# Sums for the conditioning vector: one run of four matmuls each, and units moved between stages of a four-layer trunk

## The chip, the cores and the metric

The kernel runs on one core of one Trainium2 chip. The metric is the device time of one execution in microseconds (us), the median of several runs. A core has five engines that run side by side and meet through semaphores: TensorE (PE in the profile, with its weight loads as PEld), VectorE (DVE), ScalarE (ACT), GpSimd (POOL) and SyncE (SP). SP here does nothing but issue transfers from memory, strictly in the order of the program: a transfer that must wait for a free buffer holds up all those behind it.

## The reference, cut to what matters

Four layers over 256 tokens of width 1024. Each layer has a token mixer (latent attention, causal convolution, pooling, latent attention) and a squared-ReLU MLP of width 4096. The part that the change touches is the modulation of each sub-layer by a conditioning vector `c`, called adaLN:

```
c_act = jax.nn.silu(c)
for i in range(DEPTH):
    mod = c_act @ ada_w[i] + ada_b[i]
    sh_m, sc_m, gt_m, sh_f, sc_f, gt_f = jnp.split(mod, 6, axis=-1)
    h = _rmsnorm(x, norm_g[i, 0]) * (1.0 + sc_m[:, None]) + sh_m[:, None]
    y = mixer(h)
    x = x + gt_m[:, None] * _rmsnorm(y, norm_g[i, 1])
    h = _rmsnorm(x, norm_g[i, 2]) * (1.0 + sc_f[:, None]) + sh_f[:, None]
    y = _sq_relu_mlp(h, ffn_w1[i], ffn_w2[i])
    x = x + gt_f[:, None] * _rmsnorm(y, norm_g[i, 3])
```

`ada_w` is 4 x 1024 x 6144 in float32, about 100 MB: a vector times a large matrix, once per layer, needed only when its sub-layer comes.

## The kernel before, in words

**The large products.** Weights arrive as 128 x 1024 float32 tiles (`raw`), are split into a high part (`hi`, ScalarE, L173) and a low part (`lo`, VectorE, L174), and TensorE multiplies high by high, high by low and low by high. An MLP goes through 16 chunks (`ffn`, L667): two halves of the hidden block (`h`, L652 and L655), its activation on ScalarE and VectorE (L704 to L710, which end in `gh` and `gl`), then one chunk later 24 matmuls into the output (`y`, L583, L586, L587). The last two chunks' `y` come at the end together, token tile by token tile.

**The conditioning vector.** Its weights are cut into units of 128 x 2048 (`araw`, 1 MB), eight units (k = 0 to 7) to a group, three groups to a layer; the first group is done at the start, 88 units are left. They run ahead of their use, wherever a table puts them: `MIX` and `FF` give for each sub-layer how many units go at each step or chunk, how many at the boundary ahead of it, and how many transfers are started ahead at its end. A unit is done in one of two ways (`ada`, L205):

- by TensorE (`ada_mm`, L260): four matmuls of 512 columns with 32 rows of output each, into the four quarters of one accumulator bank. All units at boundaries go this way.
- by VectorE: two multiply-adds of 128 x 1024 (L221 for the first of a group, then L223) into a pair of tiles, `acc`. All units in MLP chunks and most in the convolution go this way. The 128 partitions still have to be added up; that is one more `ada_mm`, with ones as the stationary side (`ada_flush`, L256), when the group is complete or the stage ends. I call this a sum.

When a group is complete its row is finished on VectorE (L240 to L244).

**What sets the order.** A scheduler orders the instructions of each compute engine by its own cost estimates and by the dependences. Before the change nothing ties the four matmuls of a unit or sum to each other: matmuls 0 and 1 read the first half of `acc`, 2 and 3 the second. SP's order is that of the program. There are 5 buffers for `raw`, 4 for `araw`; an `araw` buffer is free when the unit in it is summed.

**Boundaries** (L522). Between two sub-layers there is a chain: squares of `y`, a root on POOL, the residual, squares again, a root, a diagonal matrix, transposes, for token tile 0 and then tile 1. The units of the boundary are issued just after the last `y`. The wait for the second tile's `xa` (L406, L412) stands in the same chain.

**The end of an MLP.** At chunk 14 (`CF`) `ada_fetch(ahead)` starts several unit transfers in a row. After them SP issues the two tiles of `w2` for chunk 13, then those for chunks 14 and 15.

Of the kernel before, what the change touches and what calls it, by code (L numbers as in the profile page):

```python
# [51 lines left out]
def tile_trunk(ctx: ExitStack, tc: tile.TileContext, x, cT, pos, invf, ada_w, ada_bg,  # L52
# [20 lines left out]
    def bank(tag, name):  # L73
        return ps.tile([P, 512], F32, tag=tag, name=name, bufs={"y": 4, "h": 3, "ada": 1}[tag])
# [66 lines left out]
    def nosync(ins, behind):  # L141
        tc.add_manual_dep(ins.ins, behind.ins.name,
                          mybir.DependencyInfo(mybir.DependencyClass.NoSync,
                                               mybir.DependencyReason.DATA),
                          reason="after the chain")
# [58 lines left out]
    def ada(n, vec=()):  # L204
        for _ in range(n):  # L205
            if not units:
                ada_fetch(1)
            if not units:
                return
            i, g, k, raw = units.pop(0)  # L210
            if k == 0:
                grp.clear()
            if k in vec:
                ck = c_act[:, k, 0:1]
                first = "acc" not in grp
                if first:
                    grp["acc"] = sum_tiles()
                for h, acc in enumerate(grp["acc"]):
                    sl = slice(D * h, D * h + D)
                    if first:  # L220
                        V.tensor_scalar(acc, raw[:, sl], ck, None, ALU.mult)  # L221
                    else:
                        V.scalar_tensor_tensor(acc, raw[:, sl], ck, acc,  # L223
                                               op0=ALU.mult, op1=ALU.add)
            else:
                ada_mm(c_act[:, k, :], [raw[:, D * h:D * h + D] for h in range(2)],
                       k == KT - 1 and "acc" not in grp)
            if k == KT - 1:
                ada_flush(True)
                if defer[0] is None:  # L230
                    ada_row(i, g, grp["pt"])
                else:
                    defer[0].append((i, g, grp["pt"]))
# [22 lines left out]
    def ada_flush(stop=False):  # L256
        if "acc" in grp:
            ada_mm(ones_c, grp.pop("acc"), stop)

    def ada_mm(lhsT, raw, stop):  # L260
        first = "pt" not in grp
        if first:
            grp["pt"] = bank("ada", "adap")
        for j in range(4):
            mm = T.matmul(grp["pt"][32 * j:32 * j + 32, :], lhsT, raw[j // 2][:, HALF[j % 2]],
                          start=first, stop=stop)
            if gate["pe"] is not None:
                nosync(mm, gate["pe"])
        gate["ada"] = mm
# [907 lines left out]
    def pool(i, head, consts, units, ahead):  # L1177
# [87 lines left out]

    MIX = {
        0: ([2, 4, 2, 3, 3, 2], 0, 1),
        1: ([0, 0, 2, 0, 1, 2, 1, 0, 1], 2, 3),
        2: (2, 4, 3),
        3: ([0, 0, 0, 0, 0, 0], 0, 0),  # L1270
    }
    FF = {
# [3 lines left out]
        3: ([0] * NFC, 0, 0),  # L1276
    }
    qgs = cp.tile([P, q_g.shape[0], 3], F32, name="qgs")
# [139 lines left out]
```

## Time and profile before

| | us |
|---|---|
| runs shown | 1173.12, 1184.35, 1180.72 (median 1180.72) |
| the profiled execution | 1184.47 |
| its span, first to last instruction | 1182.6 |
| PE busy in the span | 1138.4 |
| DVE, ACT busy | 850.6, 645.3 |

The stages of the profiled execution: start and first attention to 150 us, MLP 0 to 342, convolution to 468, MLP 1 to 662, pooling to 690, MLP 2 to 882, second attention to 993, MLP 3 to the end. In the rows below, times are counted from the first instruction. A row of the timeline has its start, its length, engine, line, operation, output<-inputs, shape and count; what stands in brackets is the time that the engine stood idle just before, and what ended it. A float32 matmul shows as two instructions, so a sum or a unit on TensorE is "x8", half of one "x4". The end of a matmul is modelled; lengths on TensorE are therefore taken from start to start.

### The profile page before, as it was taken

How to read it: one execution, taken by the hardware profiler on the slowest of the kernel's cores; microseconds unless marked ns; L12 is line 12 of the kernel's file. 1: busy time of each engine (PE TensorE's matmuls, PEld its weight loads, DVE VectorE, ACT ScalarE, POOL GpSimd, SP SyncE). 2: the span in 40 equal slices, each digit the busy share in tenths (PEclk: the TensorE clock that was granted, in tenths of full speed). 3: DMA queues.
4: the chain of work that ended last, by engine and by line, in shares of the span. 5: the costliest groups of instructions: out<-in, count | busy, mean ns of one | idle time of the engine just before them, and what ended most of it. 6: DMA issues, size and time to landing. Idle time of an engine off the chain costs nothing. (4 is left out here: it accounts for less than half of the span.)

```text
span 1182.6 us, 17593 instructions
## 1 busy us (share of the span) xinstructions
PE 1138.4 (96%) x6706; PEld 923.5 (78%) x6706; DVE 850.6 (72%) x1197; ACT 645.3 (55%) x1145; POOL 54.1 (5%) x127
## 2 busy tenths in 40 slices
PE   7899999999999999999999999999997999999997
PEld 4667778788778867888887677878877878888886
DVE  3689787877766665787876778787876995755554
ACT  3355576556553244755564366555545675756553
POOL 1000010000010010000000110000011001000000
PEclk9999999999999988999999899999998999999999
DMA  9878759787617785778896479888644522766550
GB/s 332 304 290 311 298 208 347 270 329 290 245 53 236 256 322 213 272 272 351 315 343 256 187 278 364 311 311 323 246 134 157 170 81 80 250 199 191 183 193 35
DMA packets 73383, 290.00 MB, mean 245 GB/s; under 512 B 9986, under 2 KB 15234, under 8 KB 61012
## 3 DMA queue, kind: packets, MB, share of 16 engines
q1 hardware_dynamic: 70484, 280.44, 65.1%
q0 software_dynamic: 2816, 8.46, 2.0%
q8 instruction: 52, 0.85, 0.3%
q14 instruction: 31, 0.25, 0.1%
HBM read 286.57 MB, written 2.29 MB: 244 GB/s over the span
## 5 line engine op out<-in xcount | busy, mean ns | idle before, releaser
L174 DVE TENSOR_TENSOR lo<-raw,hi 128x1024 fp32r<-128x1024 f32 (+2 forms) x335 | 392.0, 1192 | 98.4 <-ACT hi L173 69.0
L173 ACT CAST hi<-raw 128x1024 fp32r<-128x1024 f32 (+2 forms) x335 | 335.1, 1028 | 78.6 <-PE y L587 39.4
L652 PE MATMUL h<-hT,hi 128*128 128x512 f32 x960 | 240.4, 392 | 0.0
L652 PEld LDWEIGHTS h<-hT,hi 128*128 128x128 f32 x960 | 175.8, 188 | 37.7 <-issue 3.4
L583 PE MATMUL y<-hi,gh 128*128 128x512 f32 x512 | 200.3, 393 | 1.5 <-ACT hi L173 1.5
L586 PE MATMUL y<-lo,gh 128*128 128x512 f32 x512 | 200.1, 391 | 0.2
L587 PE MATMUL y<-hi,gl 128*128 128x512 f32 x512 | 199.0, 390 | 0.0
L655 PEld LDWEIGHTS h<-hT,lo 128*128 128x128 f32 x960 | 131.0, 190 | 14.9 <-issue 5.9
L704 ACT COPY r<-h 128x256 f32<-128x256 f32 x120 | 44.5, 371 | 175.8 <-PE h L655 175.7
L655 PE MATMUL h<-hT,lo 128*128 128x256 f32 x960 | 136.0, 283 | 0.0
L223 DVE SCALAR_TENSOR_TENSOR acc<-araw,c_act,acc 128x1024 f32<-128x1024 f32 x106 | 130.7, 1279 | 0.4 <-DMA araw<-in_ada_w_dram 0.4
L583 PEld LDWEIGHTS y<-hi,gh 128*128 128x128 f32 x512 | 96.3, 188 | 22.8 <-ACT hi L173 2.4
L587 PEld LDWEIGHTS y<-hi,gl 128*128 128x128 f32 x512 | 96.1, 188 | 21.8 <-issue 0.8
L586 PEld LDWEIGHTS y<-lo,gh 128*128 128x128 f32 x512 | 96.4, 188 | 18.5 <-DVE lo L174 1.0
L705 DVE TENSOR_TENSOR r<-h,r 128x256 f32<-128x256 f32 x120 | 50.5, 421 | 39.8 <-ACT r L704 39.2
L710 DVE TENSOR_TENSOR gl<-r,gh 128x512 fp32r<-128x512 f32 x60 | 41.4, 690 | 50.2 <-ACT gh L709 50.2
L706 ACT ACTIVATE r<-r 128x512 f32<-128x512 f32 x60 | 37.9, 632 | 35.2 <-DVE r L705 35.2
L583 PE MATMUL y<-hi,hT 128*128 128x512 f32 x96 | 39.4, 412 | 0.0
L707 ACT ACTIVATE r<-r 128x512 f32<-128x512 f32 x60 | 37.9, 632 | 1.7
L586 PE MATMUL y<-lo,hT 128*128 128x512 f32 x96 | 38.8, 405 | 0.0
L587 PE MATMUL y<-hi,hT 128*128 128x512 f32 x96 | 38.6, 404 | 0.0
L709 ACT CAST gh<-r 128x512 fp32r<-128x512 f32 x60 | 37.2, 620 | 1.4
(257 smaller groups left out, 1486.8 us busy)
## 6 DMA issues: line engine op xcount, KB each, us to landing
raw<-in_w_dram SPq DMA_DIRECT2D x256, 512.0 KB, 5.8
araw<-in_ada_w_dram SPq DMA_DIRECT2D x96, 1024.0 KB, 6.4
raw<-in_w_pw_dram SPq DMA_DIRECT2D x24, 512.0 KB, 5.7
raw<-in_w_o_dram SPq DMA_DIRECT2D x16, 512.0 KB, 3.2
u<-ud SPq DMA_DIRECT2D x32, 132.0 KB, 2.8
raw<-in_w_ukv_dram SPq DMA_DIRECT2D x8, 512.0 KB
bc_g<-rowd POOLq DMA_DIRECT2D x8, 512.0 KB, 4.0
bc_a<-rowd POOLq DMA_DIRECT2D x7, 512.0 KB, 6.7
```

The source lines that it names most:

```text
L173: put(A.copy(h, raw), "act")
L174: put(V.tensor_tensor(l, raw, h.bitcast(F32), op=ALU.subtract), "dve")
L223: V.scalar_tensor_tensor(acc, raw[:, sl], ck, acc, op0=ALU.mult, op1=ALU.add)
L583: mm = T.matmul(o, ah, bh, start=start, stop=False, skip_group_check=True)
L586: T.matmul(o, ah, bl, start=False, stop=False, skip_group_check=True)
L587: return T.matmul(o, al, bh, start=False, stop=stop, skip_group_check=True)
L652: T.matmul(b, w(0, kk), pair[:, :, kk], start=(kk == 0), stop=False, skip_group_check=True)
L655: T.matmul(b[:, 0:S], w(1, kk), pair[:, 0, kk], start=False, stop=(kk == KT - 1), skip_group_check=True)
L704: A.copy(rf, hb[:, S:])
L705: V.tensor_tensor(rf, hb[:, 0:S], rf, op=ALU.add)
L706: A.activation(r, r, AF.Relu)
L710: gli = V.tensor_tensor(gl, g2, gh.bitcast(F32), op=ALU.subtract)
```

## The change

Two things. In `ada_mm` the four matmuls go in the order 2, 3, 0, 1, and each is tied behind the one before it, so that the scheduler keeps that order. And the table gives other numbers of units:

| | before | after |
|---|---|---|
| MLP 0, chunks (VectorE) | 15 | 17 |
| boundary into the convolution (TensorE) | 2 | 1 |
| convolution, its steps (VectorE) | 6 | 7 |
| convolution, after its taps (TensorE) | 1 | 0 |
| boundary into MLP 1 (TensorE) | 2 | 1 |
| MLP 1, chunks (VectorE) | 17 | 21 |
| boundary into the pooling, pooling (TensorE) | 4, 2 | 4, 2 |
| boundary into MLP 2 (TensorE) | 2 | 1 |
| MLP 2, chunks (VectorE) | 20 | 17 |

So 4 of the 88 units go from TensorE to VectorE. Since the groups now end elsewhere, the number of sums goes from 11 to 13: a new one at the end of MLP 0 and one at the end of the convolution. The numbers of transfers started ahead are as before.

```
         first = "pt" not in grp
         if first:
             grp["pt"] = bank("ada", "adap")
-        for j in range(4):
+        mm = None
+        for j in (2, 3, 0, 1):
+            prev = mm
             mm = T.matmul(grp["pt"][32 * j:32 * j + 32, :], lhsT, raw[j // 2][:, HALF[j % 2]],
                           start=first, stop=stop)
+            if prev is not None:
+                nosync(mm, prev)
             if gate["pe"] is not None:
                 nosync(mm, gate["pe"])
         gate["ada"] = mm
...
     FF = {
...
-        1: ([1, 1, 1, 2, 1, 1, 2, 1, 1, 2, 1, 1, 1, 1, 0, 0], 2, 4),
+        1: ([2, 1, 1, 2, 1, 2, 1, 2, 1, 2, 1, 2, 1, 2, 0, 0], 1, 4),
```

The lines of the new file from L272 on are four higher (L652 becomes L656), and L265 becomes L267.

TensorE, MLP 2, the last sum of the kernel (`adap<-acc`), ahead of the hidden block of chunk 15; before:

```order
L652 MATMUL h_8215<-hT,hi 128x512 x8
L655 MATMUL h_8215<-hT,lo 128x256 x6
L265 MATMUL adap<-acc,ones_c 32x512 x2
L655 MATMUL h_8215<-hT,lo 128x256 x2
L265 MATMUL adap<-acc,ones_c 32x512 x2
L652 MATMUL h_8234<-hT,hi 128x512 x8
```

and now:

```order
L656 MATMUL h_8217<-hT,hi 128x512 x6
L267 MATMUL adap<-acc,ones_c 32x512 x4
L656 MATMUL h_8217<-hT,hi 128x512 x2
L659 MATMUL h_8217<-hT,lo 128x256 x8
L656 MATMUL h_8236<-hT,hi 128x512 x8
```

The two pairs have become one run of four, which stands 8 matmuls earlier in the hidden block. All 13 sums now stand in runs of four; before, 9 of 11 were split.

ScalarE, the same place, from the activation of chunk 13 (`gh`) to that of chunk 14 (`hi` are weight tiles); before:

```order
L709 CAST gh<-r 128x512
L173 CAST hi<-raw 128x1024 x4
L704 COPY r<-h_8110 128x256
L173 CAST hi<-raw 128x1024
L704 COPY r<-h_8129 128x256
L706 ACTIVATE r<-r 128x512
L173 CAST hi<-raw 128x1024
L707 ACTIVATE r<-r 128x512
L173 CAST hi<-raw 128x1024
L709 CAST gh<-r 128x512
```

and now:

```order
L713 CAST gh<-r 128x512
L173 CAST hi<-raw 128x1024
L708 COPY r<-h_8112 128x256
L173 CAST hi<-raw 128x1024 x2
L708 COPY r<-h_8131 128x256
L710 ACTIVATE r<-r 128x512
L711 ACTIVATE r<-r 128x512
L713 CAST gh<-r 128x512
```

Seven weight casts stood between the two activations, three stand there now; none is left between the last `r` and `gh`.

SP, MLP 1, from the units of chunk 13 on (`araw` are units, `raw` MLP weights; `DVE_49` is a wait for VectorE); before:

```order
L197 DMA araw<-in_ada_w_dram 128x2048 x2
L200 DMA bg<-in_ada_bg_dram 4x1024 [waits DMAHW7_49]
L197 DMA araw<-in_ada_w_dram 128x2048 [waits DMAHW0_49,DVE_49]
L197 DMA araw<-in_ada_w_dram 128x2048 [waits DMAHW1_49,DVE_49]
L155 DMA raw<-in_w_dram 128x1024 [waits DMAHW2_49,Activation_49]
L155 DMA raw<-in_w_dram 128x1024 [waits DMAHW3_49,Activation_49]
```

and now:

```order
L197 DMA araw<-in_ada_w_dram 128x2048
L197 DMA araw<-in_ada_w_dram 128x2048 [waits DMAHW3_49,DVE_49]
L197 DMA araw<-in_ada_w_dram 128x2048 [waits DMAHW4_49,DVE_49]
L197 DMA araw<-in_ada_w_dram 128x2048 [waits DMAHW5_49,DVE_49]
L155 DMA raw<-in_w_dram 128x1024 [waits DMAHW6_49,Activation_49]
L155 DMA raw<-in_w_dram 128x1024 [waits DMAHW7_49,Activation_49]
```

Four transfers ahead as before. The last waits for the last unit of chunk 13 to be summed; that chunk had one unit and now has two.

## Rows read from the trace of the kernel before

**Rows 1.** The page, part 1: busy time of each engine.

```profile
PE 1138.4 (96%) x6706; PEld 923.5 (78%) x6706; DVE 850.6 (72%) x1197; ACT 645.3 (55%) x1145; POOL 54.1 (5%) x127
```

**Rows 2.** Groups by line, TensorE, units and sums: busy, mean ns, idle before.

```profile
L265 PE MATMUL adap<-araw,c_act 128*32 128x512 f32 x192 | 29.1, 607 | 0.0
L265 PE MATMUL adap<-acc,ones_c 128*32 128x512 f32 x88 | 21.9, 603 | 1.7 <-DVE acc L223 1.7
```

**Rows 3.** Timeline of TensorE, MLP 0, a sum in two pairs.

```profile
220.45 0.63 PE L652 MATMUL h<-hT,hi 128*128 128x512 f32 x2
221.02 1.05 PE L265 MATMUL adap<-acc,ones_c 128*32 128x512 f32 x4
...
222.67 1.05 PE L265 MATMUL adap<-acc,ones_c 128*32 128x512 f32 x4
223.65 0.73 PE L652 MATMUL h<-hT,hi 128*128 128x512 f32 x2
```

**Rows 4.** Timeline, the same place: VectorE's last units, TensorE's hidden block ahead.

```profile
217.30 4.87 DVE L223 SCALAR_TENSOR_TENSOR acc<-araw,c_act,acc 128x1024 f32<-128x1024 f32 x4
...
217.69 1.98 PE L652 MATMUL h<-hT,hi 128*128 128x512 f32 x8
219.50 0.76 PE L655 MATMUL h<-hT,lo 128*128 128x256 f32 x5
```

**Rows 5.** Timeline of TensorE, two sums that waited (MLP 0, MLP 2).

```profile
310.40 1.05 PE L265 MATMUL adap<-acc,ones_c 128*32 128x512 f32 x4 [0.69 <-DVE acc L223]
...
867.04 1.05 PE L265 MATMUL adap<-acc,ones_c 128*32 128x512 f32 x4 [0.98 <-DVE acc L223]
```

**Rows 6.** Timeline of TensorE, boundaries into MLP 0, convolution and MLP 2.

```profile
150.00 1.07 PE L265 MATMUL adap<-araw,c_act 128*32 128x512 f32 x8
150.99 0.48 PE L381 MATMUL hT_ps<-pick,shT 40*128 40x512 f32 x1
...
340.43 1.92 PE L265 MATMUL adap<-araw,c_act 128*32 128x512 f32 x16
342.29 0.48 PE L381 MATMUL hT_ps<-pick,shT 40*128 40x512 f32 x1
...
691.88 1.16 PE L395 MATMUL hT_ps<-dg,xa 128*128 128x128 f32 x8 [1.20 <-ACT dg L389]
```

**Rows 7.** Timeline of TensorE, the unit after the convolution's taps.

```profile
436.16 1.44 PE L265 MATMUL adap<-araw,c_act 128*32 128x512 f32 x8
437.53 0.79 PE L1143 MATMUL y<-hi,ones_r 1*128 1x512 f32 x1
```

**Rows 8.** Timeline, end of MLP 1: SP, VectorE, ScalarE and TensorE.

```profile
623.21 9.17 SPq L197 DMA_DIRECT2D araw<-in_ada_w_dram  x2
629.55 2.48 DVE L223 SCALAR_TENSOR_TENSOR acc<-araw,c_act,acc 128x1024 f32<-128x1024 f32 x2
632.48 12.87 SPq L155 DMA_DIRECT2D raw<-in_w_dram  x8
638.52 1.03 ACT L173 CAST hi<-raw 128x1024 fp32r<-128x1024 f32 x1
639.60 1.19 PE L583 MATMUL y<-hi,gh 128*128 128x512 f32 x4 [1.52 <-ACT hi L173]
```

**Rows 9.** Timeline, end of MLP 2: TensorE's hidden block, VectorE's last unit.

```profile
863.37 1.98 PE L652 MATMUL h<-hT,hi 128*128 128x512 f32 x8
...
865.71 2.47 DVE L223 SCALAR_TENSOR_TENSOR acc<-araw,c_act,acc 128x1024 f32<-128x1024 f32 x2
```

**Rows 10.** Stretches: PE, PEld, DVE, ACT, POOL busy; clock, DMA share, GB/s.

```profile
760.00:850.00 90.00, 90.00 (x460) 75.31 (x459) 74.06 (x82) 51.19 (x76) 0.00 (x0) 1.00 0.85 321
437.00:450.00 13.00, 13.00 (x37) 8.38 (x34) 6.84 (x14) 6.36 (x17) 1.17 (x2) 0.50 0.89 359
...
890.00:895.00 5.00, 4.45 (x21) 3.88 (x22) 3.73 (x12) 3.49 (x10) 2.22 (x4) 0.66 0.33 84
```

**Rows 11.** Timeline of TensorE, boundary into the second attention.

```profile
890.55 2.17 PE L412 MATMUL hT_ps<-ident,xa 128*128 128x128 f32 x8 [3.62 <-DVE xa L406]
```

More of the change, by code (lines that the diff above doesn't have):

```diff
@@ L263, in ada_mm @@
             grp["pt"] = bank("ada", "adap")
-        for j in range(4):
+        mm = None
+        for j in (2, 3, 0, 1):
+            prev = mm
             mm = T.matmul(grp["pt"][32 * j:32 * j + 32, :], lhsT, raw[j // 2][:, HALF[j % 2]],
                           start=first, stop=stop)
+            if prev is not None:
+                nosync(mm, prev)
             if gate["pe"] is not None:
@@ L1267, in tile_trunk @@
         0: ([2, 4, 2, 3, 3, 2], 0, 1),
-        1: ([0, 0, 2, 0, 1, 2, 1, 0, 1], 2, 3),
+        1: ([0, 0, 2, 0, 1, 2, 1, 1, 0], 1, 3),
         2: (2, 4, 3),
```

6 rows, old and new, of the table FF are left out of this document.

## The prediction

> **What bounds the kernel.** I read the page first, then the groups by line, then TensorE's timeline stage by stage, and last the other engines at the places where TensorE stands. TensorE shows 96% busy, VectorE 72%, ScalarE 55% [rows 1]. The idle 44 us of TensorE are spread over the start, the two attentions and the boundaries; inside an MLP it hardly stands at all. There a matmul less is time won, and work on VectorE costs nothing until TensorE has to wait for it. So the change is counted in TensorE's own time, and VectorE, SP and the transfers only where they come last.
>
> One number sets the scale: all units and sums on TensorE show 29.1 + 21.9 = 51 us [rows 2]. 192 instructions are 24 units, 88 are 11 sums, so a unit shows 1.2 us and a sum 2.0. The sum is dearer because most sums are split. A pair lasts as long as a run of four: 221.02 to the next matmul is as long as a whole unit, 150.00 to 150.99, and two units take 1.86 [rows 3, 6]. Four quarters go side by side, and half of them save nothing.
>
> **The change, part by part**, in us of the profiled execution.
>
> *Sums joined in the MLPs.* From 220.45 to 223.65 stand four hidden-block matmuls and one sum in two pairs [rows 3]. Eight such matmuls take 217.69 to 219.50, 0.23 each [rows 4], so the two runs cost 3.20 - 4 x 0.23 = 2.28, with what it costs to get in and out, and one run 1.14. Seven MLP sums are split (MLP 0 two, MLP 1 two of three, MLP 2 three) and become one run each: 7 x 1.14 = **-8.0**. The two attention sums and the one among the convolution's taps are interleaved with other small work and I take 0 for them, between -1 and +1 together.
>
> *Waits at these sums.* With the second half first, the whole run waits for VectorE's last multiply-add; before, the first pair could go 1.24 earlier. Two runs waited, 0.69 and 0.98 [rows 5]. That in MLP 0 moves to a place 8 matmuls of the short kind later: -0.7. The first in MLP 0 now stands after six matmuls of 217.69, at 219.05; its group now ends with the first unit of that chunk, at 217.30 + 2.48 = 219.78, so it can wait 0.7 [rows 4]: I take +0.4, half, since that chunk's VectorE work also has one weight tile less ahead of it. The last one in MLP 2 is the doubtful one: after six matmuls of 863.37, TensorE comes to it at 864.73, and the sum was ready at 865.71 + 2.47 = 868.18 [rows 9], a wait of 3.45 where it was 0.98. But that unit was late because `gh` stood behind late weight casts on ScalarE, and in the new order none is left between `r` and `gh`, and they are tiles fetched earlier. I leave this wait at 0.98 and keep -1 to +2.5 as its bounds. The rest have VectorE ready within 0.2. Together **-0.3**.
>
> *New sums.* One at the end of MLP 0, one among the last taps: 2 x 1.14 = **+2.3**.
>
> *Units taken out of boundaries.* A second unit costs 1.86 - 0.99 = 0.87 [rows 6]. In the boundaries into the convolution and MLP 1 nothing stands behind it but TensorE's own chain, and the wait that follows (0.75 in either) is the same with one unit and with two. So 2 x -0.87 = **-1.7**. In the boundary into MLP 2 the next matmul waits 1.20 for the diagonal [rows 6]; a unit less only makes that wait longer: **0**. The unit after the taps took 436.16 to 437.53 [rows 7]; part of it covered the layer norm on VectorE: **-1.0**, bounds -1.4 and 0.
>
> *Work moved to VectorE.* Each unit is 2.47 [rows 9]; MLP 1 gets four, 10 us on top of 145 busy in 184. Its densest chunks become one and a half units per chunk throughout. Exactly that density stands in chunks 4 to 13 of MLP 2 before, 15 units in ten chunks: there TensorE is busy 90.00 of 90 us, with the transfers at 0.85 of their share [rows 10]. So 0.
>
> *The transfer queue at the end of MLP 1.* Here the change adds a wait. SP sends four units ahead, and the fourth needs the last unit of chunk 13 summed: two transfers take 9.17 to issue from 623.21, until VectorE's unit of 629.55 ends at 632.0. Only then, at 632.48, come the weights of the second matrix for chunk 13; they are cast at 638.52 and TensorE waits 1.52 for them [rows 8]. With two units in that chunk VectorE ends 2.48 later, so do the issue, the cast and TensorE: **+2.5**, bounds 0 (the chunk's activation comes earlier by as much) and +5 (it comes later by as much). Queued behind it are only MLP 1's last weights and the pooling's, with 20 us to spare.
>
> Sum: -8.0 - 0.3 + 2.3 - 1.7 - 1.0 + 2.5 = **-6.2**. On the profiled 1184.5 that is 1178.3. This execution stands 3.8 above the median of the runs shown, so I forecast 1180.7 - 6.2 = **1174.5**.
>
> **Rivals.** I call within 1% what a measurement of this kernel can hardly tell from no change; 1% is 11.8 us.
>
> A, *TensorE stands at the ones* (about -1, 1179.5). Each joined run waits for the later half; with 1.24 or so at three of the seven and the 3.45 of MLP 2 instead of 0.98, 5 to 6 us come back. For it: both waits of [rows 5] are of this kind, and nothing of TensorE's later work filled them. The Trainium skill, "TensorE: Matmul & The Clock Gate", section on packing small matmuls, says that matmuls are strict in order, without reordering; by that rule such a wait stands in full, and the trace agrees with its 0.69 and 0.98. Against it: five of the seven are met by a sum that was ready. 17%.
>
> B, *a long stretch at half clock goes away* (1167.5). TensorE runs at 0.50 of its clock from 437 to 450 [rows 10], just after the convolution's taps, which is 1.2 instead of 2.4 GHz and costs 6.5 us; the pooling has one of 10 us. The change takes work out of TensorE just at 436.16. If one of these is gone the time is 1174.5 - 7 = 1167.5. For it: the runs shown differ by 11 us with the same program. Against: taps, transposes and rank-one matmuls, which it was doing when the clock fell, stay. 21%.
>
> C, *slower, by SP's queue in MLP 1*. The price is the length of the block: if chunk 13's activation is itself late, because two units also stand in chunk 11, the block of 9.17 comes a second time instead of 2.5, +6.7; and a wait of such a length can be followed by half clock, as the 3.62 at 890.55 was: 890 to 895 was granted 0.66 [rows 10, 11]. With a stretch like that of 437 to 450 (6.5) it is 1174.5 + 13.2 = 1187.7. It decides from a wait of 7.7 at the first output matmul of chunk 13, where the gain is spent. The Trainium skill says on the same page, in its part on HAM oscillation, that gaps between matmul bursts bring the lower clock back; by that rule the new wait is charged twice, as at 890.55, while the 1.52 of [rows 8] was not followed by a fall here. For C: TensorE already waits there. Against: [rows 10], the same density without a wait. 8%, of which 3% beyond 1%.
>
> D, *the change does not do what it says*: the order shows all 13 sums in runs of four and the units where the table puts them. 2%, 1181.
>
> **How the numbers follow.** The forecast has 52%, A 17%, B 21%, C 8%, D 2%. Range: the forecast's own bounds, -1.4 for the convolution, 0 for SP's queue and -1 for the last sum, give about 1170.5 below; with a shorter fall of the clock as well it is B's, 1165. Above, +2.5 at SP and +2.5 at the last sum, with +1 in the attentions, give 1180.5; A lies within, and 1184 takes in half of C. So 1165 to 1184. Faster by over 1% (below 1168.9) is B, 21%; slower by over 1% is the far end of C, 3%; the rest is 76%.
>
> **What would show it.** In the changed profile the sums should be 104 instructions with a busy time near 14 instead of 21.9, the units 160 instead of 192. Each step: seven single runs of about 1.0 with their waits written beside them, above all the last one in MLP 2 (0 to 1 us by the forecast, over 3 by A); 0.99 instead of 1.86 in two boundaries, and a longer wait for the diagonal into MLP 2 (about 2); at the end of MLP 1 the second SP stretch of `raw` some 2.5 later after chunk 13's `gl`, and a wait near 4 at the first `y`. The forecast is wrong if waits for `acc` add up to over 3 us, if that wait at `y` exceeds 7, if weights come late elsewhere in MLP 1, or if stretches at half clock come or go.

## The result

The change makes the kernel slower: median 1195.3 us (1191.17 to 1199.15) against 1179.5 before (four runs of each), ratio 1.013, 95% interval 1.0086 to 1.0175. Two runs of the changed kernel lie near 1191 and two near 1199, so a difference to its median is good to some 5 us. 1174.5 was forecast, 1165 to 1184 as its range; "slower by over 1%" had 3%. The profiled execution of the changed kernel has a span of 1197.4 us (1182.6 before).

The matmuls that are not units or sums are the same 6426 in both traces, in the same order up to neighbours. So the start of one and the same matmul cuts both traces into stages (us from cut to cut; the cuts are the stage ends named ahead of the prediction):

| | MLP 0 | convolution | MLP 1 | pooling | MLP 2 | the rest | sum |
|---|---|---|---|---|---|---|---|
| before | 191.3 | 125.8 | 194.1 | 28.0 | 192.0 | 444.8 | 1175.9 |
| changed | 188.2 | 141.8 | 199.5 | 24.1 | 191.8 | 445.3 | 1190.7 |
| difference | -3.1 | **+16.0** | **+5.4** | -3.9 | -0.2 | +0.6 | +14.8 |

(The units of the boundaries into the convolution and MLP 2 lie ahead of the cut, those of the boundaries into MLP 1 and the pooling behind it. Rounded, so that a sum may be 0.1 off.) MLP 0 gains about what was forecast. The loss is in the convolution and at the end of MLP 1, and inside MLP 2's -0.2 a gain of 4.6 among the chunks meets a loss of 4.4 at the boundary. The pooling's -3.9 goes with a stretch at half clock that it had before (672.2 to 682.5) and has no longer.

The page of the changed kernel, part 1, and the groups of units and sums (columns as in [rows 1] and [rows 2]):

```profile
PE 1135.2 (95%) x6690; PEld 929.6 (78%) x6690; DVE 857.7 (72%) x1205; ACT 644.1 (54%) x1145; POOL 55.1 (5%) x127
...
L267 PE MATMUL adap<-araw,c_act 128*32 128x512 f32 x160 | 25.5, 601 | 0.0
L267 PE MATMUL adap<-acc,ones_c 128*32 128x512 f32 x104 | 15.6, 639 | 2.5 <-DVE acc L223 2.5
```

TensorE is busy 3 us less and the span is 15 longer: the time is in waits and in what they do to the clock. 13 sums take 15.6 where 11 took 21.9. The one wait for `acc` is 2.46, and it is not in an MLP.

**The convolution's end**, timeline of the changed kernel (SP, POOL, TensorE and VectorE; the unit, the sum and the taps that the new table puts there):

```profile
421.52 1.01 POOL L324 DMA_DIRECT2D bc_g<-rowd  x1 [0.84 <-DMA rowd<-row]
421.56 2.40 SPq L1083 DMA_DIRECT2D u<-ud  x4
422.52 0.54 POOL L324 DMA_DIRECT2D bc_a<-rowd  x1
424.01 1.19 SPq L197 DMA_DIRECT2D araw<-in_ada_w_dram  x1
425.30 2.43 SPq L1083 DMA_DIRECT2D u<-ud  x4
431.14 3.23 PE L1064 MATMUL dw_ps<-u,dg 128*32 128x128 f32 x64 [6.37 <-DMA u<-ud]
435.08 2.48 DVE L223 SCALAR_TENSOR_TENSOR acc<-araw,c_act,acc 128x1024 f32<-128x1024 f32 x2 [10.11 <-DMA araw<-in_ada_w_dram]
437.70 1.94 PE L267 MATMUL adap<-acc,ones_c 128*32 128x512 f32 x8 [2.46 <-DVE acc L223]
```

And the same place before:

```profile
417.75 3.73 SPq L1079 DMA_DIRECT2D u<-ud  x8
423.09 1.09 PE L1060 MATMUL dw_ps<-u,dg 128*32 128x128 f32 x32
...
429.99 0.57 POOL L320 DMA_DIRECT2D bc_g<-rowd  x1 [4.55 <-DMA rowd<-row]
```

`u` is the input of the taps, written to memory and read back in another layout. Before, its last eight reads were issued in one go and the taps followed 1.6 us behind the last. Now the transfer of the unit moved from behind the taps to the last step stands between the two sets of four and takes 1.19 to issue. And since one more unit is done ahead of the convolution (two more in MLP 0, one fewer at the boundary), the group ends a step earlier, its row goes out earlier, and the two broadcasts of it (512 KB each) now run beside `u`. TensorE waits 6.37, then 2.46 more at the new sum, whose unit landed only then. Half clock begins within the first wait and comes again later (windows of the changed kernel; last columns: clock, DMA share, GB/s):

```profile
427.00:434.00 7.00, 2.86 (x60) 2.89 (x64) 0.00 (x0) 0.00 (x0) 0.00 (x0) 0.51 1.04 259
451.00:464.50 13.50, 12.85 (x34) 8.71 (x33) 7.89 (x15) 6.93 (x16) 1.16 (x2) 0.50 0.29 117
```

**The end of MLP 1**, which answers to [rows 8]:

```profile
630.21 17.81 SPq L197 DMA_DIRECT2D araw<-in_ada_w_dram  x4
642.20 0.68 DVE L714 TENSOR_TENSOR gl<-r,gh 128x512 fp32r<-128x512 f32 x1
642.80 4.86 DVE L223 SCALAR_TENSOR_TENSOR acc<-araw,c_act,acc 128x1024 f32<-128x1024 f32 x4
648.11 2.50 SPq L155 DMA_DIRECT2D raw<-in_w_dram  x4
654.88 1.04 ACT L173 CAST hi<-raw 128x1024 fp32r<-128x1024 f32 x1 [3.98 <-DMA raw<-in_w_dram]
655.98 1.22 PE L587 MATMUL y<-hi,gh 128*128 128x512 f32 x2 [6.92 <-ACT hi L173]
```

The changed kernel is 10.98 late when it comes here. With that taken off, chunk 13's `gl` is 2.3 later than before (628.95 there), VectorE's last unit ends 4.65 later (2.3 + 2.4 for the second unit), SP goes on 4.65 later, the cast is 5.4 later, and TensorE waits 6.92 instead of 1.52. From within the wait, half clock is granted (columns as above):

```profile
652.30:662.50 10.20, 6.48 (x14) 4.63 (x15) 6.12 (x5) 6.19 (x6) 0.00 (x0) 0.50 0.97 355
```

**The boundary into MLP 2**, which answers to the last row of [rows 6]:

```profile
692.51 1.18 POOL L321 DMA_DIRECT2D rowd<-row  x2
698.07 0.57 POOL L324 DMA_DIRECT2D bc_g<-rowd  x1 [4.38 <-DVE hT L1233]
704.16 1.29 DVE L518 TENSOR_TENSOR v<-y,bc_g 128x512 f32<-128x512 f32 x2 [3.09 <-DMA bc_g<-rowd]
709.27 0.94 PE L399 MATMUL hT_ps<-dg,xa 128*128 128x128 f32 x6 [3.58 <-ACT dg L393]
```

The wait for the diagonal is 3.58, with about 2 forecast. The row's broadcast is issued 5.6 behind the row (2.0 before: 677.34 and 679.35), and VectorE waits 3.09 for it. But counted from the last matmul of MLP 1 the transposes with the diagonal start at 28.2, before at 29.7: TensorE comes to them earlier, since the pooling is 3.9 shorter, and gives that back in the wait and in the half clock around it. Pooling and boundary together lose 0.5.

### The profile page after: what moved, and what is told of

It reads as the page before. It is cut to its first block, busy times and chain, and to the rows that moved or that the text cites. A ratio compares the mean times of both kernels' runs of the same rounds, so it can differ in the third digit from the quotient of the medians.

```text
span 1197.4 us, 17582 instructions
## 1 busy us (share of the span) xinstructions
PE 1135.2 (95%) x6690; PEld 929.6 (78%) x6690; DVE 857.7 (72%) x1205; ACT 644.1 (54%) x1145; POOL 55.1 (5%) x127
## 5 line engine op out<-in xcount | busy, mean ns | idle before, releaser
L656 PE MATMUL h<-hT,hi 128*128 128x512 f32 x960 | 240.7, 392 | 0.0
L656 PEld LDWEIGHTS h<-hT,hi 128*128 128x128 f32 x960 | 175.6, 188 | 37.7 <-issue 3.4
L223 DVE SCALAR_TENSOR_TENSOR acc<-araw,c_act,acc 128x1024 f32<-128x1024 f32 x110 | 135.7, 1278 | 10.1 <-DMA araw<-in_ada_w_dram 10.1
L587 PE MATMUL y<-hi,hT 128*128 128x512 f32 x96 | 39.6, 413 | 0.6 <-DVE hT L1162 0.6
L1064 PE MATMUL dw_ps<-u,dg 128*32 128x256 f32 (+1 forms) x640 | 32.4, 355 | 7.8 <-DMA u<-ud 7.3
L518 DVE TENSOR_TENSOR v<-y,bc_g 128x512 f32<-128x512 f32 x32 | 21.9, 688 | 24.6 <-ACT junk L135 21.5
```

The costliest lines, as they stand in the source:

```text
L223: V.scalar_tensor_tensor(acc, raw[:, sl], ck, acc, op0=ALU.mult, op1=ALU.add)
L587: mm = T.matmul(o, ah, bh, start=start, stop=False, skip_group_check=True)
L656: T.matmul(b, w(0, kk), pair[:, :, kk], start=(kk == 0), stop=False, skip_group_check=True)
```

## The experiments

My theory at this point: the run of four is worth what the forecast gave it, and the table costs at three places where SP or the way to memory holds something that TensorE needs.

**The run of four alone, and the table alone.** The first kernel is the changed one with both tables of before; the second is the kernel before with both new tables.

> The run of four alone, with the table of before. My theory now: the run of four is worth what the forecast gave it, and the loss comes from the table, at two places where SP's queue holds a transfer that TensorE needs. Then the split sums of the MLPs become one run each, 7 x 1.14 = 8 us less: 1171 to 1173 against 1179.5, no wait for acc over 1.5 us. Rival: the run of four is what costs, because TensorE stands at the ones until the later half is summed: then this kernel is level with before or slower (1179 to 1190).

> The new table alone, with the four matmuls of a sum left untied. My theory: both holds of the queue stay (a wait near 6 us at the last taps, near 7 at the first output matmul of chunk 13 of MLP 1), and the MLP sums cost a second run again, some 8 x 1.14 = 9 us: 1202 to 1206. Rival (the run of four costs): 1180 to 1190.

Measured: 1169.3 (ratio 0.993, 0.990 to 0.996), 2 below its range, and 1203.6 (1.020, 1.017 to 1.024). Both rivals fall: the run of four gains, the table alone loses 24. In the second trace the two waits are there, and with matched matmuls it is 11.8 longer than the changed kernel; 9.5 of that are eight places of 1.14 to 1.21, seven in MLPs and one in the convolution's steps, where a sum stands in two pairs. Waits of the table alone, timeline of TensorE:

```profile
436.59 3.64 PE L1060 MATMUL dw_ps<-u,dg 128*32 128x128 f32 x64 [7.22 <-DMA u<-ud]
664.61 1.22 PE L583 MATMUL y<-hi,gh 128*128 128x512 f32 x2 [6.76 <-ACT hi L173]
```

and the sums of the run of four alone (as [rows 2]; 11 sums of 1.14 now):

```profile
L267 PE MATMUL adap<-acc,ones_c 128*32 128x512 f32 x88 | 12.6, 604 | 1.6 <-DVE acc L223 1.6
```

Whether the tie alone, with the matmuls in the order 0 to 3, would do as much was not run.

**The end of MLP 1: the transfers ahead put behind the weights.**

```
-                if c == CF:
+                if c == CF and i != 1:
                     ada_fetch(ahead)
...
                     rowblock([w2[i, 2 * cc + k] for k in range(2)], ...)
+                if c == CF and i == 1:
+                    ada_fetch(ahead)
```

> The changed kernel, with the four transfers that MLP 1 starts ahead issued behind the weights of the second matrix for chunk 13, instead of in front of them; the table is that of the changed kernel. My theory (place in the queue): the wait of 6.92 at chunk 13's first output matmul is gone (below 1) and so is the half clock of 652 to 662; the pooling may get back its own stretch at half clock that before had (672 to 682, 5 us). So 5 to 11 us less: 1184 to 1190. Rival (density): VectorE with 21 units is too late with the weight tiles; then a wait of 4 or more stays there, 1192 to 1196.

Measured: 1186.4 (to before 1.0066, 1.0041 to 1.009), 8.9 less than the changed kernel; MLP 1 takes 191.2 instead of 199.5. This holds across kernels: with the table's MLP 1 and the run of four it takes 198.8 to 199.5 in six kernels without this edit and 191.2 to 191.9 in three with it. Same table, same units on VectorE, so its density is not the cause. Timeline of that kernel, the queue (all six weight tiles ahead of the four units) and the stretch (clock, DMA share, GB/s last):

```profile
617.57 17.81 SPq L155 DMA_DIRECT2D raw<-in_w_dram  x6
635.42 10.00 SPq L197 DMA_DIRECT2D araw<-in_ada_w_dram  x4
...
640.00:655.00 15.00, 13.58 (x69) 10.07 (x68) 11.45 (x14) 5.63 (x9) 0.00 (x0) 1.00 0.96 376
```

No wait is left at that `y`; one of 1.38 comes 8 us later, and the clock stays at 2.4 GHz.

**The convolution, step by step.** Three lists of units for its eight steps and the place behind the taps:

```
-        1: ([0, 0, 2, 0, 1, 2, 1, 1, 0], 1, 3),      # changed kernel
+        1: ([0, 0, 2, 0, 1, 2, 2, 0, 0], 1, 3),      # conv_step6
+        1: ([0, 0, 1, 0, 1, 2, 2, 0, 0], 1, 3),      # conv_late_row; MLP 1's boundary 1 -> 2
+        1: ([0, 0, 1, 0, 1, 2, 1, 0, 1], 1, 3),      # conv_before;   MLP 1's boundary 1 -> 2
```

> The changed kernel, with the unit of the convolution's last step done in the step before: its transfer leaves the place between the two last sets of u. The row's broadcast (two transfers of 512 KB, issued at 421.5 as in the changed kernel) stays where it is. My theory (place in the queue): the wait of 6.37 at the last taps falls below 1.5, the wait of 2.46 at the sum falls, and with them most of the half clock that follows: 10 to 13 us less, 1182 to 1186 against 1195.3. Rival (broadcast): u is late because the broadcast now runs at the same time; then a wait of 4 or more stays, 1190 to 1194.

> conv_step6 with the group that ends in the convolution ending one step later, as before: its row is sent as in the kernel before, behind the last u (one unit fewer in the third step, one more at the boundary into MLP 1, +0.9). conv_step6 kept a wait of 2.74 at the sum, one of 2.22 at the taps and a stretch at half clock of 10.2 us from 419, with the row's two transfers of 512 KB on the way together with u. My theory now: the loss in the convolution is two things in one place, the queue position (conv_step6 took that away: 1195.3 to 1190.7) and the row's transfers that share the way with u. Then u lands within 2 us of its last issue, TensorE waits under 1.5 there in all, and the half clock of 419 to 429 goes or moves: 1182 to 1186. Rival: it is the two unit transfers just ahead of u that fill the way; these stay, and with them 1189 to 1193.

> The changed kernel with the convolution's units as before (six on VectorE, none begun behind the row, one on TensorE after the taps; two at the boundary into MLP 1). No sum is left at the end of the convolution then. conv_late_row had u in time, but TensorE stood 2.67 at the new sum ahead of the last taps. My theory: this sum is the third part of the loss; without it no wait over 1.5 us is left at the last taps, and the convolution is 12 to 15 us shorter than in the changed kernel, less 1.9 for the two units put back: 1180 to 1184, with less in the slowest runs. Rival (the half clock behind the taps comes whatever is waited for): level with conv_late_row, 1184 to 1188, and a stretch of 10 us or more at half clock behind the taps.

Measured: 1190.7, 1184.3 and 1178.8 (the last to before: 1.0002, 0.9985 to 1.002); conv_late_row is in its range, conv_before 1 below its own. In the same order, TensorE's waits at that place, for conv_step6 with POOL's broadcasts and SP's `u` ahead:

```profile
414.55 0.81 POOL L324 DMA_DIRECT2D bc_g<-rowd  x1 [1.05 <-DMA rowd<-row]
415.39 0.54 POOL L324 DMA_DIRECT2D bc_a<-rowd  x1
414.37 4.95 SPq L1083 DMA_DIRECT2D u<-ud  x8
420.34 1.93 PE L267 MATMUL adap<-acc,ones_c 128*32 128x512 f32 x8 [2.74 <-DVE acc L223]
424.49 3.64 PE L1064 MATMUL dw_ps<-u,dg 128*32 128x128 f32 x64 [2.22 <-issue]
```

```profile
426.33 1.42 PE L267 MATMUL adap<-acc,ones_c 128*32 128x512 f32 x8 [2.67 <-DVE acc L221]
427.45 2.86 PE L1064 MATMUL dw_ps<-u,dg 128*32 128x128 f32 x48
```

```profile
419.57 1.97 PE L1064 MATMUL dw_ps<-u,dg 128*32 128x128 f32 x64 [1.15 <-DMA u<-ud]
```

The place in the queue alone did not do it: conv_step6 missed its range (its time lies in the rival's), and its `u`, issued in one go by 419.3, still came only at 424.5, with the row's broadcasts issued at 414.6 and 415.4. With the row behind `u` (conv_late_row) nothing waits for `u`. The DMA packets of `u` in the traces settle what holds it: from the issue of the write ahead of it to the landing of its last part it takes 6.4 to 7.1 in all seven kernels whose row goes out behind `u`, 12.3 in conv_step6, where the row goes ahead of it, and 14.4 to 17.6 in the five that have the unit between its two sets as well. The two unit transfers just ahead of `u`, the rival, are still there in conv_late_row (6.7), so it falls. What stays is the new sum, which stands in front of the last taps in TensorE's order while VectorE finishes the row and begins the next group. Without that sum the convolution is as before: 122.2 in conv_before, 121.4 with the run of four alone, 125.8 before (which has the 13.7 of half clock of [rows 10]). The rival of conv_before falls: no half clock follows its taps.

How much each of the three is worth can't be read closely. The convolution of the changed kernel stands unchanged in mlp1_behind, where it took 140.3 with a wait of 7.86 at the taps, and in mlp2_two and pool_none below, where it took 133.4 and 133.1 instead of 141.8, with the same wait at the taps (6.13 and 6.34). Of the difference to these two some 4 is a wait of 2.38 at 372 for weights that landed late, with half clock behind it, and most of the rest half clock behind the taps. conv_step6's 132.8 is hardly below these two; conv_late_row's 130.1 is 3 below. The sum's part is the clearest: 130.1 and 131.1 (all_undone below) with it, 122.2 and 121.9 (table_repaired below) without it.

**The boundary into MLP 2.** One unit moved back from MLP 2 to the boundary; then the pooling's two units moved to MLP 2.

```
-        2: (2, 4, 3),                    # MIX
+        2: (0, 4, 3),                    # pool_none; MLP 2 17 -> 19
...
-        2: ([1, 1, 1, 1, 1, 1, 1, 1, 1, 1, 2, 1, 1, 2, 1, 0], 1, 0),
+        2: ([1, 1, 1, 1, 1, 1, 1, 1, 1, 1, 2, 1, 1, 1, 1, 0], 2, 0),     # mlp2_two
```

> The changed kernel with two units again at the boundary into MLP 2 (one fewer in MLP 2). The changed kernel waits 3.58 for the diagonal there, before 1.20, and is granted half clock from 700 to 703 and 710 to 717, which before it was not. My theory: the second unit fills that wait and keeps the clock; the boundary gives back some 4 us: 1190 to 1193 against 1195.3. Rival (the forecast's 0, a unit there hides in the wait either way): 1195 to 1197.

> The changed kernel without the two units of the pooling (two more in MLP 2, on VectorE). In the changed kernel the row of the boundary into MLP 2 is sent at 692.5, while five unit transfers and four weight tiles issued from 682.5 to 690.6 are on their way, and its broadcast is issued 5.6 us later (2.0 before); VectorE then waits 3.09 for bc_g and TensorE 3.58 for the diagonal, with half clock around it. My theory (the row shares the way with transfers that nobody waits for): two transfers fewer, the wait for bc_g falls below 1 and that of TensorE below 2, the half clock of 700 to 717 shrinks; with the two units themselves (1.9) 5 to 9 us less: 1186 to 1190. Rival (the row's way is not the cause): the wait stays over 3, and 1192 to 1195.

Measured: 1194.3 and 1192.1 against 1195.3; neither shows a gain, and neither is in its theory's range. In mlp2_two VectorE waits 6.47 for `bc_g` and TensorE 7.47, so the second unit fills nothing. (Where that boundary is as in the changed kernel the wait is not one number either: 6.26, 6.32 and 6.62 in conv_step6, conv_late_row and conv_before.) In pool_none the wait for `bc_g` is gone, as forecast, and TensorE's is what it was, which was not:

```profile
689.08 0.57 POOL L324 DMA_DIRECT2D bc_g<-rowd  x1 [2.85 <-issue]
694.44 1.28 DVE L518 TENSOR_TENSOR v<-y,bc_g 128x512 f32<-128x512 f32 x2
699.54 0.80 PE L399 MATMUL hT_ps<-dg,xa 128*128 128x128 f32 x2 [3.57 <-ACT dg L393]
```

So two things hold the diagonal up: the row, and the chain itself, which lasts 5.4 from the last square of the first token tile to the diagonal (693.69 to 699.09; before 686.03 to 691.43, where two units on TensorE covered part of it). Each repair was tried alone, and each leaves the other. Both together were not run.

**The repairs together.** all_undone joins conv_late_row, mlp1_behind and mlp2_two; table_repaired joins conv_before, mlp1_behind and pool_none; run_behind is the run of four with the table of before and mlp1_behind's edit.

> The three repairs together: the convolution as in conv_late_row, MLP 1's transfers ahead behind the weights of chunk 13, two units at the boundary into MLP 2. If the three places hold the whole loss and add up (9 from MLP 1, 10 to 13 from the convolution, 4 from the boundary), 1169 to 1173, level with the run of four alone (1169.3). Rival: the table costs elsewhere too (density of VectorE): 1176 or more.

> The run of four with the table of before, and MLP 1's four transfers ahead behind the weights of chunk 13. There TensorE waits only 1.54 for these weights. Theory (the hold's price is the wait that it makes): 1 to 2 us less than the run of four alone, 1167 to 1169. Rival (moving the transfers ahead back makes the units at the pooling late and costs there): 1170 to 1175.

> conv_before, pool_none and mlp1_behind together: the table of the change for the MLPs, with the three holds away. If the three places carry the loss: 1195.3 - 13 - 6 - 9 = 1167, and 1164 to 1170 with the boundary units saved, level with or just better than the run of four alone (1169.3). Rival (the table costs elsewhere too, as all_undone with 1180 can be read): 1173 or more.

Measured: 1180.1, 1168.8 (ratio 0.9906, 0.9887 to 0.9924) and 1170.5 (0.9934, 0.9911 to 0.9958). all_undone missed by 7 or more: it still had the new sum's wait in the convolution (131.1 for the stage, with 17 us at half clock from 434, some 14 behind that wait) and 5.94 for the diagonal. That pointed at the sum, and conv_before followed from it. table_repaired ends within 0.5 of the range that the sum of its parts gave. It is 24.8 below the changed kernel, and conv_before and mlp1_behind alone give 16.5 and 8.9: the convolution and the end of MLP 1 carried the loss.

Beside run_behind the units that table_repaired still has moved bring nothing: TensorE waits 4.12 for the diagonal in it. run_behind's own gain over the run of four alone (0.5) is within what the runs differ by; MLP 1 is 3 shorter, and the boundary into MLP 2 gives that back (a wait of 4.43 for `xa`, where the run of four alone waits 1.11 for the diagonal). Both beat the kernel before, by 0.9% and 0.7%, and nearly all of it is the run of four.

## Why the prediction was wrong

- *Sums joined, -8.0*: right. 1.14 to 1.21 for each of the eight in table_only, 8.4 by the ratio of run_only.
- *Waits at these sums, -0.3*: within its bounds, and better. No sum in an MLP waits in the changed kernel, the doubtful one in MLP 2 neither, so the 0.69 and 0.98 are both gone. With the table of before (run_only) two sums still wait, 0.52 and 1.04.
- *New sums, +2.3*: MLP 0's is +1.2. The convolution's is mis-sized: it takes 1.94 at half clock and waits 2.46. It was priced as work; in TensorE's order it stands ahead of the last taps and waits for a unit that has just been fetched.
- *Units out of boundaries, -1.7 and 0*: right for the first two (0.6, since the wait behind it grew by 0.3, and 0.9); wrong for MLP 2's, which lost 4.4. The forecast took the wait there as one that only a unit's 0.87 could move; the row's way to VectorE was not looked at, nor that a shorter pooling ahead of it, 3.9 here, only makes TensorE wait longer.
- *The convolution's unit, -1.0*: **the step that failed.** The stage lost 16.0 in the profiled execution; it takes 133 to 142 in the four kernels with this list and the run of four, 120 to 126 in the five whose list ends as before. The price given was that of the four matmuls taken off TensorE. What the new table puts into the other queues was taken as nothing: the unit's transfer goes from behind the taps into the middle of the last `u`; with one more unit ahead of the convolution the group's end, its row and the row's broadcasts come a step earlier, beside `u`; and the units begun behind the group's end need the new sum ahead of the last taps. conv_before takes these three back and is 16.5 less by the medians. SP's order shows the first (one `araw` between two sets of four `u`), and the lists of units give the second. No rival stood at this place.
- *Work moved to VectorE, 0*: right. From 558 to 620, in the denser chunks of MLP 1, TensorE has no idle time in the changed kernel, and mlp1_behind shows the same.
- *SP's queue at the end of MLP 1, +2.5*: right in mechanism, wrong in size and bounds. The second unit is 2.4, as worked out; chunk 13's activation came 2.3 later: four casts now stand between its steps on ScalarE (none before), which makes `gh` 1.7 later, and a `lo` on VectorE ahead of `gl` gives the rest; the weights were 0.7 longer on their way. That is 5.4, just above the upper bound. The matmuls are 10.98 late ahead of the wait and 18.89 behind it, so the half clock from 652.3 to 662.5 adds 2.5 and the place cost 7.9.

Rival C had this queue, the sign and the half clock, but only with a wait of 7.7 or more, and 8%. With 7.9 in place of 2.5 the forecast would still have read 1179.9; the convolution was in none of the cases. Rival A's strict order held, but the only sum that waited is the new one. Rival B's half clock went the other way: it adds up to some 68 us in the changed kernel, to 38 before. The Trainium skill, "TensorE: Matmul & The Clock Gate", in its part on HAM oscillation, says that gaps between matmul bursts bring the lower clock back; by that rule each of the two long waits is charged twice, and the trace agrees (0.51 and 0.50, from within each wait to 2.7 and 6.5 us behind its end). The stretch from 451 to 464 has no such wait right ahead.

## What to carry to other kernels

When a table moves a step, write down for every queue what that step issues and what is issued right behind it; here a transfer, a row and a sum that came to stand elsewhere cost a stage some 16 us, for 1 us of work taken off TensorE. A row moves with the count of units ahead of it, so a table can be changed in one stage and lose in the next. What is fetched ahead belongs behind the last transfer that the running stage needs, in this kernel a move of two lines worth 8.9 us in the medians, 8.2 in the stage. And count a sum that ends a group as a point where TensorE meets the other engine, not only as work: where nothing independent can stand in front of it in the order, it makes all that is behind it wait.

## What the runs showed of the hardware

- Four matmuls into four quarters of the output rows in one run take 0.98 to 1.00 from start to start at full clock, and two pairs twice that; the second run costs 1.14 to 1.21, at eight places (table_only against the changed kernel).
- With eight reads of `u` of 132 KB issued in one go, the taps could start 1.6 behind the last issue before, and only 5.2 behind it in conv_step6, beside the row's two broadcasts of 512 KB; the issues themselves took 3.7 and 5.0. From the issue of the write ahead of them to the last landing it took 6.4 before and 12.3 in conv_step6.
- The same convolution, with a wait of 6.1 to 7.9 at the taps, took 133 to 142 us, above all by its half clock (stretches of 6.8, 3.4 and 3.4 in mlp2_two, of 10.2, 3.4 and 10.2 in mlp1_behind, of 3.4, 6.8, 3.4 and 13.7 in the changed kernel). What decides this stays open; one profile of such a stage is good to some 8 us.
